# Weight sums of a seven-product multiplication made by adding DMA transfers: one decoder layer on one core

## The chip, the cores and the metric

The kernel runs on one core of a Trainium2 chip. A core has five engines with a queue of instructions each: TensorE (PE, matrix products into PSUM), VectorE (DVE), ScalarE (ACT), GpSimd (POOL) and SyncE (SP), and 16 DMA engines that they share. SP and POOL start the DMA transfers in this kernel. The metric is the device time of one execution in microseconds (us); lower is better.

## What is computed

One decoder layer on 512 tokens of 2048 features, in float32. A normed input is projected to 6664 features; three groups work on these (a convolution, a "forgetting" attention of 8 heads, a memory attention of 4 heads); their gated outputs, 2048 features together, go through the output projection, a residual and a norm.

```python
h = rmsnorm(x, norm_g[l])
proj = h @ w_in[l]
(cv_a, cv_b, cv_gate, fq, fk, fv, f_logit, fox_gate, mq, mem_gate) = jnp.split(proj, SPLITS, axis=-1)
...
y_fox = fox_attention(fq.reshape(shp), fk.reshape(shp), fv.reshape(shp), logf)   # causal, 8 heads of 128
y_fox = y_fox * jax.nn.silu(fox_gate)
...
y = jnp.concatenate([y_conv, y_fox, y_mem], axis=-1)
x = x + y @ w_out[l]
return rmsnorm(x, final_g)
```

## The kernel before

PE multiplies reduced float32 (`F32R`), which keeps too few bits, so each operand is split into a high and a low part: `split` casts on ACT (line 93, `whi`) and takes the remainder on DVE (line 94, `wlo`). A product of two operands is then three matmuls (high x high, high x low, low x high). `operand` does this for a weight tile `raw` of [128, 8, 128] floats (512 KB), with three buffers for each of `whi` and `wlo` and six for `raw`.

The stages follow one another: the start (memory keys and values, norm, transposes of `h`), the convolution and the memory attention, then the eight heads of the forgetting attention, then the output projection.

**The pair stage.** A head needs four blocks of 128 features, worked on as two pairs: query and key, then gate and value. The first pair (`plain_pair`) is multiplied as it is. The other 15 (`pair`, lines 711 to 759) use Winograd's form of Strassen's scheme: the 2x2 block product of weights (two feature blocks `fa`, `fb` by two halves of the 2048 rows) and `h` (two halves of the features by two halves of the tokens) is done in seven half-size products instead of eight. Each of the seven (`product`) is 24 matmuls of 256 columns on sums of blocks. The sums of `h`'s quarters, `s1` to `s4`, are made once (`first_sums`, `last_sum`). The sums of weights are made for every pair: four plain loads on SP's queue (line 719) fetch the blocks `b11`, `b12`, `b22`, `b21`, and `less` (line 703) takes four differences on DVE. The three PSUM tiles `x1`, `zo`, `x2` gather the results: a product adds onto what lies in its tile, and between products DVE adds to a tile (`plus`, line 700) or ACT copies it away (`kept`, line 707).

A pair is a generator of three steps. The main loop runs a pair's first step, then the previous pair's last product and attention work, then the pair's second step, so that attention overlaps the next pair's products. A scheduler that the framework runs at build time orders each engine's queue by its own estimates; what it did is shown with the change. Attention's masks (line 796) run on POOL, which also starts the DMA that writes a head's finished output `yd` (line 833).

**The output steps.** The output projection works by eight steps, `STEPS`: four "y" steps (plain products of the convolution's and the memory's parts) and four "s" steps (`heads`, the heads' parts in the same seven-product form, with sums of `y`'s quarters made by `head_ys`). An "s" step loads four tiles of `w_out` (`next_piece`) and takes the same four differences on DVE by line 703. Its matmuls are line 981; results are added onto `res` by `add` (line 907).

Of the kernel before, what the change touches and what calls it, by code (L numbers as in the profile page):

```python
# [17 lines left out]
P = 128  # L18
S = 512
# [28 lines left out]
def hybrid_layer_kernel(  # L48
# [41 lines left out]
    def split(hi, lo, src, scale=None):  # L90
        """hi + lo == src (times scale): twelve significant bits each."""
        if scale is None:
            ins = nc.scalar.copy(hi, src)  # L93
            nc.vector.tensor_tensor(lo, src, hi.bitcast(F32), ALU.subtract)  # L94
        else:
            ins = nc.scalar.activation(hi, src, AF.Identity, scale=scale)
            nc.vector.scalar_tensor_tensor(
                lo, src, scale, hi.bitcast(F32), ALU.mult, ALU.subtract
            )
        return ins.ins  # L100
# [6 lines left out]

    bg = deque()
# [8 lines left out]
    def operand(src, out=None):  # L117
        """src [P, n, c], whole -> its two parts."""
        if out is None:
            out = tuple(  # L120
                wp.tile(list(src.shape), F32R, tag=t, name=nm(t), bufs=3) for t in ("whi", "wlo")
            )
        split(*out, src)
        return out

    def weights(src, n, c, raw=None, hold=None):
        """src [n * P, c] -> k -> (hi, lo) of its k-th P rows."""
        half = n // 2
# [23 lines left out]
    # x normed, [feature, token], two features' tiles in each  # L152
# [12 lines left out]
    # ---- start: memory values and keys (rows transposed as they come, their  # L165
    # norm applied to the results), x normed and transposed ----
# [130 lines left out]
    def project(f0, per=0):  # L297
        """[P features from f0, tokens] in PSUM."""
        w = weights(w_in[:, f0 : f0 + P], KT, P)
        o = pj()  # L300
        for k in range(KT):
            mm3(o, w(k), (h_hi[k], h_lo[k]), k == 0, k == KT - 1)
        background(per)
        return o

    def silu_of(pool, o, tag, bufs):
        """silu of a PSUM tile."""
        sg = pool.tile([P, S], F32, tag=tag, name=nm(tag), bufs=bufs)
# [5 lines left out]
    NC = CW // P  # L314
    PAD = TAPS - 1
    with tc.tile_pool(name="conv", bufs=1, reuse_waits="tile") as cp:
# [151 lines left out]
        with tc.tile_pool(name="matt", bufs=1, reuse_waits="tile") as ma:  # L468
            # the channel norm's sums and the gates run between the heads
# [68 lines left out]
        # sums of h's quarters (token halves by feature halves); the last takes  # L538
        # the place of the quarter that no product needs
# [22 lines left out]
        def first_sums(g):  # L562
            t1, t2, t3 = tmp("t1"), tmp("t2"), tmp("t3")
            whole(t1, quarter(g, 0, 1))
            whole(t2, quarter(g, 1, 1))
            nc.vector.tensor_tensor(t2, t1, t2, ALU.add)
            split(*sums[0][g], t2)
            whole(t3, quarter(g, 0, 0))
            nc.vector.tensor_tensor(t1, t3, t1, ALU.subtract)
            split(*sums[2][g], t1)  # L570
            nc.vector.tensor_tensor(t2, t2, t3, ALU.subtract)
            split(*sums[1][g], t2)

        def last_sum(g, t1, t2):
            whole(t1, quarter(g, 1, 0))
            whole(t2, sums[1][g])
            nc.vector.tensor_tensor(t1, t1, t2, ALU.subtract)
            split(*quarter(g, 0, 1), t1)
# [18 lines left out]
    # ---- the output projection's operands; what they need of the room of h and  # L597
    # its sums falls free with the last pair's products. The convolution's and
    # the memory's parts of y are multiplied as they are; the heads' parts by the
    # same form as the pairs, with sums of their quarters (token halves by halves  # L600
    # of the heads) ----
# [14 lines left out]
    def w_pieces():  # L616
        for kind, n in STEPS:
            c0 = n * S
            if kind == "s":
                for k0, c in ((4, c0), (4, c0 + M), (8, c0 + M), (8, c0)):  # L620
                    yield w_rows(k0, HK, c, M), HK, M
            else:
                for k0 in (0, 2, 12, 14):
                    yield w_rows(k0, 2, c0, S), 2, S
# [33 lines left out]
    def head_ys(j, fa, fb):  # L658
        """Heads j and 4 + j, whole: their quarters' parts and those of the
        sums, which take the room of fa and fb."""  # L660
# [15 lines left out]
        nc.vector.tensor_tensor(a22, a21, a22, ALU.add)  # L676
        split(*q["s1"], a22)
        nc.vector.tensor_tensor(a22, a22, a11, ALU.subtract)
# [3 lines left out]
        nc.vector.tensor_tensor(a12, a12, a22, ALU.subtract)  # L682
# [4 lines left out]
    with tc.tile_pool(name="fox", bufs=1, reuse_waits="tile") as fx:  # L687
# [14 lines left out]
        def less(o, p, q):  # L702
            nc.vector.tensor_tensor(o, p, q, ALU.subtract)  # L703

# [5 lines left out]
        def pair(fa, fb):  # L710
            """Features fa.. and fb.., P each, by Winograd's form of Strassen's
            seven products: the first in PSUM, by token halves, the second in
            SBUF. In three steps, for another pair's to come between."""
            HK = KT // 2

            def load(f0, half):
                r = raw_tile(HK, P)
                rows = slice(half * HK * P, (half + 1) * HK * P)
                nc.sync.dma_start(
                    out=r, in_=w_in[rows, f0 : f0 + P].rearrange("(k p) f -> p k f", p=P)  # L720
                )
                return r

            # Sums are taken in PSUM: a product adds onto what its bank holds,
            # which copies and an addition have read or changed before. Only a
            # bank's first product starts afresh.
# [10 lines left out]
            b11, b12, b22, b21 = load(fa, 0), load(fb, 0), load(fb, 1), load(fa, 1)  # L737
            x1, zo, x2 = (pj((P, M)) for _ in range(3))
            product(x1, b11, a11, start=True)
            yield  # L740
            p1 = kept(x1, "p1")
            less(b11, b12, b11)
            product(zo, b11, s1, start=True)
            p5 = kept(zo, "p5")
            less(b11, b22, b11)
            product(x2, b11, s2, start=True)
            plus(x2, x2, p1)
            u2 = kept(x2, "u2")
            product(x1, b21, a12)
            product(zo, b22, s4)  # L750
            less(b12, b22, b12)
            product(x2, b12, s3)
            col = fx.tile([P, S], F32, tag="col", name=nm("col"), bufs=2)
            plus(col[:, M:], x2, p5)
            plus(col[:, :M], zo, u2)
            less(b21, b21, b11)
            yield
            product(x2, b21, a22)
# [130 lines left out]
    head_ys(3, heads[6], last_y)  # L889
    with tc.tile_pool(name="outp", bufs=1, reuse_waits="tile") as op:  # L890
# [4 lines left out]
        # by token halves and column blocks  # L895
# [12 lines left out]

        ALL = slice(0, S)
# [9 lines left out]
        def sides(n):  # L919
            """y's other parts; the last time, a token tile at a time and to the end."""  # L920
# [20 lines left out]
            for t in range(NT):  # L941
# [3 lines left out]
                # the very last one by halves, for less to follow its products  # L945
# [40 lines left out]
        def heads(n):  # L986
            b11, b12, b22, b21 = (next_piece() for _ in range(4))
            x1, zo, x2 = (pj((P, 2, M)) for _ in range(3))
            r11, r12, r21, r22 = (
                res[h][n][:, :, c * M : (c + 1) * M] for h in range(2) for c in range(2)  # L990
            )
            product(x1, b11, "a11", start=True)
            yield
            p1 = y_room(n % 2).rearrange("p (t f) -> p t f", f=M)
            nc.scalar.copy(p1, x1)
            less(b11, b12, b11)
            product(zo, b11, "s1", start=True)
            add(r22, zo)
            less(b11, b22, b11)
            product(x2, b11, "s2", start=True)  # L1000
            add(x2, p1)
            add(r12, x2)
            product(zo, b22, "s4")
            add(r12, zo)
            less(b12, b22, b12)
            product(x1, b21, "a12")
            add(r11, x1)
            product(x2, b12, "s3")
            add(r22, x2)
            less(b21, b21, b11)  # L1010
            yield
            product(x2, b21, "a22")
            add(r21, x2)
# [66 lines left out]
```

## Time and profile before

| what | value |
|---|---|
| median of 3 runs | 870.68 us (870.58 to 870.77) |
| the profiled execution: span, first to last instruction | 868.8 us |
| PE busy | 855.3 us (98%) |
| DVE busy | 704.8 us (81%) |
| ACT busy | 436.2 us (50%) |
| POOL busy | 45.1 us (5%) |
| hardware DMA queue | 102.52 MB, 39.3% of 16 engines |
| software DMA queue (POOL's) | 4.11 MB, 1.3% of 16 engines |
| granted TensorE clock | 0.996 |

The profiled execution's own device time isn't listed apart from the runs; beside its span of 868.8 us stands their median. In the rows of the profile, "L703 DVE TENSOR_TENSOR raw<-raw,raw" is an instruction of line 703 on DVE that reads two `raw` tiles and writes one; "x76 | 92.7, 1220 | 0.5" is 76 of them, 92.7 us busy, 1220 ns each, 0.5 us of idle time of the engine before them. Rows of waits read "who waits <- for what: us in total, times, longest". A DMA's "took" is the issue on its engine; "to landing" is from issue to the arrival of the data. A row of windows gives start and end, the length, then each engine's busy time, the granted clock, the mean busy share of the DMA engines and GB/s.

### The profile page before, as it was taken

To read this page: it belongs to the slowest core of one execution; us is meant where nothing else is said; L and a number is where in the kernel's file an instruction comes from. 1 tells how busy PE (TensorE), PEld (TensorE's weight loads), DVE (VectorE), ACT (ScalarE), POOL (GpSimd) and SP (SyncE) were. 2 spreads that over 40 slices of the span, in tenths; PEclk is the share of its full clock that TensorE was granted. 3 is DMA by queue.
4 is the path that set the end of the run, shared out by engine and by line. 5 is a ranking of instruction groups with operands and counts; after the bars stand their busy time and mean duration, and the time that the engine had idled before them with its cause. 6 is when DMAs were issued, how large, how long until landed. Compare 5 with 4: busy or idle time off the path is not lost.

```text
span 868.8 us, 14045 instructions
## 1 busy us (share of the span) xinstructions
PE 855.3 (98%) x5562; PEld 775.1 (89%) x5562; DVE 704.8 (81%) x1051; ACT 436.2 (50%) x679; POOL 45.1 (5%) x76
## 2 busy tenths in 40 slices
PE   8999999999999999999999999999999999999996
PEld 6897887888888888999999999999999888998995
DVE  4686799999977998998787878878797886876964
ACT  4874322224346544566565555656464852443523
POOL 1011000000000002010101010101010000000001
PEclk9999999999999999999999999999999999999999
DMA  9972233333332333233434243333334627351415
GB/s 323 356 197 76 70 82 105 97 97 89 94 85 85 109 90 117 79 106 109 121 93 127 74 120 101 107 103 91 107 84 146 239 73 267 97 195 49 146 49 194
DMA packets 143265, 107.52 MB, mean 124 GB/s; under 512 B 3892, under 2 KB 126816, under 8 KB 142560
## 3 DMA queue, kind: packets, MB, share of 16 engines
q1 hardware_dynamic: 141696, 102.52, 39.3%
q0 software_dynamic: 1504, 4.11, 1.3%
q8 instruction: 43, 0.70, 0.3%
q14 instruction: 22, 0.18, 0.1%
HBM read 98.46 MB, written 8.14 MB: 123 GB/s over the span
## 4 chain that ended last, share of the span: by engine, by line
PE 95%; issue 1%; ACT 1%; DVE 1%; DMA 1%; SPq 0%; POOL 0%; POOLq 0%; ACTq 0%
PE pj L732 33%; PE pj L104 13%; PE pj L105 13%; PE pj L106 13%; PE pj L981 8%; PE at L104 3%; PE at L105 3%; PE at L106 3%; PE at L820 1%; DMA raw<-in_w_mem_kv_dram 1%; PE pj L409 0%; PE pj L408 0%; PE pj L262 0%; PE at L262 0%; PE at L782 0%
## 5 line engine op out<-in xcount | busy, mean ns | idle before, releaser
L93 ACT CAST whi<-raw 128x1024 fp32r<-128x1024 f32 x205 | 215.1, 1051 | 324.2 <-PE pj L105 110.9
L94 DVE TENSOR_TENSOR wlo<-raw,whi 128x1024 fp32r<-128x1024 f32 x205 | 250.1, 1221 | 87.5 <-ACT whi L93 86.6
L105 PE MATMUL pj<-hl,whi 128*128 128x512 f32 x352 | 139.6, 397 | 0.0
L106 PE MATMUL pj<-hh,wlo 128*128 128x512 f32 x352 | 139.1, 396 | 0.0
L104 PE MATMUL pj<-hh,whi 128*128 128x512 f32 x352 | 138.9, 396 | 0.0
L732 PE MATMUL pj<-hh,wlo 128*128 128x256 f32 x480 | 135.0, 281 | 0.0
L732 PE MATMUL pj<-hl,whi 128*128 128x256 f32 x480 | 134.9, 281 | 0.0
L732 PE MATMUL pj<-hh,whi 128*128 128x256 f32 x480 | 134.8, 281 | 0.0
L703 DVE TENSOR_TENSOR raw<-raw,raw 128x1024 f32<-128x1024 f32 x76 | 92.7, 1220 | 0.5
L732 PEld LDWEIGHTS pj<-hl,whi 128*128 128x128 f32 x480 | 90.4, 188 | 0.1
L732 PEld LDWEIGHTS pj<-hh,whi 128*128 128x128 f32 x480 | 90.5, 188 | 0.0
L732 PEld LDWEIGHTS pj<-hh,wlo 128*128 128x128 f32 x480 | 90.4, 188 | 0.0
L329 DVE SCALAR_TENSOR_TENSOR acc<-up,cwt,acc 128x512 f32<-128x512 f32 x120 | 85.2, 741 | 0.4
L981 PE MATMUL pj<-whi,rh 128*128 128x256 f32 x448 | 80.0, 280 | 0.7 <-DVE sst L1035 0.4
L104 PEld LDWEIGHTS pj<-hh,whi 128*128 128x128 f32 x352 | 66.1, 188 | 15.9 <-PE pj L262 0.2
L106 PEld LDWEIGHTS pj<-hh,wlo 128*128 128x128 f32 x352 | 66.1, 188 | 15.7
L105 PEld LDWEIGHTS pj<-hl,whi 128*128 128x128 f32 x352 | 66.1, 188 | 15.5
L981 PEld LDWEIGHTS pj<-whi,rh 128*128 128x128 f32 x448 | 68.8, 188 | 1.3 <-DVE res L907 1.1
L981 PE MATMUL pj<-wlo,rh 128*128 128x256 f32 x224 | 62.3, 279 | 0.0
L981 PEld LDWEIGHTS pj<-wlo,rh 128*128 128x128 f32 x224 | 42.1, 188 | 0.2
L796 POOL TENSOR_SCALAR_AFFINE_SELECT b<-b 128x128 f32<-128x128 f32 x32 | 21.3, 676 | 265.6 <-ACT b L795 234.0
L732 PE MATMUL pj<-s0h,whi 128*128 128x256 f32 x120 | 34.9, 291 | 0.0
(302 smaller groups left out, 1720.5 us busy)
## 6 DMA issues: line engine op xcount, KB each, us to landing
raw<-in_w_in_dram SPq DMA_DIRECT2D x104, 512.0 KB, 3.6
raw<-in_w_out_dram SPq DMA_DIRECT2D x32, 512.0 KB, 4.5
raw<-in_w_mem_kv_dram SPq DMA_DIRECT2D x12, 512.0 KB, 7.3
xr<-in_x_dram SPq DMA_DIRECT2D x4, 1024.0 KB, 7.8
res<-in_x_dram SPq DMA_DIRECT2D x8, 512.0 KB, 6.8
out_dram<-res SPq DMA_DIRECT2D x16, 256.0 KB, 2.8
rs<-yd SPq DMA_DIRECT2D x15, 256.0 KB, 4.6
mr<-in_mem_dram SPq DMA_DIRECT2D x8, 256.0 KB, 7.2
```

The costliest lines, as they stand in the source:

```text
L93: ins = nc.scalar.copy(hi, src)
L94: nc.vector.tensor_tensor(lo, src, hi.bitcast(F32), ALU.subtract)
L104: nc.tensor.matmul(o, ah, bh, start=start, stop=False)
L105: nc.tensor.matmul(o, ah, bl, start=False, stop=False)
L106: nc.tensor.matmul(o, al, bh, start=False, stop=stop)
L329: return lambda: nc.vector.scalar_tensor_tensor(a, up[:, j : j + S], cwt[:, c, j : j + 1], a, ALU.mult, ALU.add)
L703: nc.vector.tensor_tensor(o, p, q, ALU.subtract)
L732: nc.tensor.matmul(o, p[:, k, :], q, start=start and k == 0 and i == 0, stop=k == HK - 1 and i == 2, skip_group_check=True,)
L796: nc.gpsimd.affine_select(out=b[:, sl], in_=b[:, sl], pattern=[[-1, P]], compare_op=ALU.is_ge, fill=MASKED, base=0, channel_multiplier=1,)
L820: nc.tensor.transpose(tp[:, (i - j) * P : (i - j + 1) * P], pr[i][:, j * P : (j + 1) * P], ident)
L981: nc.tensor.matmul(o[:, m, :], p, q[:, k, :], start=start and k + m + i == 0, stop=k == HK - 1 and i == 2, skip_group_check=True,)
```

## The change

The sums of weights are no longer made on DVE. A tile is loaded plainly, and then further blocks are fetched by DMA transfers that add onto it in SBUF (`accum_op=ALU.add`, on POOL's queue). Since only adding is used, all weight sums have plus signs: one tile, `chain`, is in turn the first block, plus a second, plus a third, plus a fourth; another, `r22`, gets one addition. The signs of the sums of `h` and `y` and of some PSUM steps change to match (`negated_less`, `take`). Blocks that were loaded once and used in several sums are fetched anew for each sum: beside 60 plain loads of the pairs (line 726 after) come 60 adding ones (line 730 after), beside 16 of the output steps 16 more (line 1003 after). The products are reordered: from a11, s1, s2, a12, s4, s3, a22 to s1, a11, s4, s2, a12, s3, a22, so that between two uses of the chain's tile lie products that use other tiles. `less` is gone. The number of PE's instructions is the same.

```diff
+    def negated_less(o, p, q):
+        nc.vector.scalar_tensor_tensor(o, p, -1.0, q, ALU.mult, ALU.subtract)
...
-            nc.vector.tensor_tensor(t2, t1, t2, ALU.add)
+            nc.vector.tensor_tensor(t2, t2, t1, ALU.subtract)
...
-                for k0, c in ((4, c0), (4, c0 + M), (8, c0 + M), (8, c0)):
+                for k0, c in ((4, c0), (4, c0), (8, c0 + M), (8, c0)):
...
         def pair(fa, fb):
+            def rows(f0, half):
+                r = slice(half * HK * P, (half + 1) * HK * P)
+                return w_in[r, f0 : f0 + P].rearrange("(k p) f -> p k f", p=P)
...
+            def plus_weights(r, f0, half):
+                nc.gpsimd.dma_start(out=r, in_=rows(f0, half), accum_op=ALU.add)
...
-            b11, b12, b22, b21 = load(fa, 0), load(fb, 0), load(fb, 1), load(fa, 1)
+            chain, r11 = load(fa, 0), load(fa, 0)
+            plus_weights(chain, fb, 0)
+            r22, r21 = load(fb, 1), load(fa, 1)
             x1, zo, x2 = (pj((P, M)) for _ in range(3))
-            product(x1, b11, a11, start=True)
+            product(zo, chain, s1, start=True)
             yield
+            plus_weights(chain, fb, 1)
+            p5 = kept(zo, "p5")
+            product(x1, r11, a11, start=True)
             p1 = kept(x1, "p1")
-            less(b11, b12, b11)
-            product(zo, b11, s1, start=True)
-            p5 = kept(zo, "p5")
-            less(b11, b22, b11)
-            product(x2, b11, s2, start=True)
+            product(zo, r22, s4)
+            plus_weights(r22, fb, 0)
+            product(x2, chain, s2, start=True)
+            plus_weights(chain, fa, 1)
             plus(x2, x2, p1)
             u2 = kept(x2, "u2")
-            product(x1, b21, a12)
-            product(zo, b22, s4)
-            less(b12, b22, b12)
-            product(x2, b12, s3)
             col = fx.tile([P, S], F32, tag="col", name=nm("col"), bufs=2)
-            plus(col[:, M:], x2, p5)
-            plus(col[:, :M], zo, u2)
-            less(b21, b21, b11)
+            negated_less(col[:, :M], zo, u2)
+            product(x1, r21, a12)
+            product(x2, r22, s3)
+            negated_less(col[:, M:], x2, p5)
             yield
-            product(x2, b21, a22)
+            product(x2, chain, a22)
             yield (x1, x2), col
...
         def heads(n):
-            b11, b12, b22, b21 = (next_piece() for _ in range(4))
+            chain, r1, r2, r3 = (next_piece() for _ in range(4))
+            c0 = n * S
+
+            def plus_weights(r, k0, c):
+                nc.gpsimd.dma_start(out=r, in_=w_rows(k0, HK, c, M), accum_op=ALU.add)
...
+            plus_weights(chain, 4, c0 + M)
+            product(zo, chain, "s1", start=True)
+            take(r22, zo)
             yield
+            plus_weights(chain, 8, c0 + M)
+            product(x1, r1, "a11", start=True)
...
+            product(zo, r2, "s4")
+            take(r12, zo)
+            plus_weights(r2, 4, c0 + M)
+            product(x2, chain, "s2", start=True)
+            plus_weights(chain, 8, c0)
             add(x2, p1)
-            add(r12, x2)
...
+            take(r12, x2)
+            product(x1, r3, "a12")
             add(r11, x1)
-            product(x2, b12, "s3")
-            add(r22, x2)
-            less(b21, b21, b11)
+            product(x2, r2, "s3")
+            take(r22, x2)
             yield
-            product(x2, b21, "a22")
+            product(x2, chain, "a22")
             add(r21, x2)
```

First place: POOL's queue in the pair stage, about one head (two pairs) of it. Before, it holds a head's four masks and the write of the head's output:

```order
L796 AFFINE_SELECT b_4190<-b_4190 128x128
L796 AFFINE_SELECT b_4206<-b_4206 128x128
L796 AFFINE_SELECT b_4222<-b_4222 128x128
L796 AFFINE_SELECT b_4238<-b_4238 128x128
L833 DMA yd_68<-fgate_3906 128x512
```

After, the same queue; `raw_4408` is the chain of a pair of queries and keys and `raw_4413` its `r22`, `raw_4111` and `raw_4116` are those of the pair before, `raw_4680` and `raw_4977` the chains of the next two:

```order
L730 DMA raw_4408<-in_w_in_dram 128x8x128
L730 DMA raw_4111<-in_w_in_dram 128x8x128
L730 DMA raw_4116<-in_w_in_dram 128x8x128
L730 DMA raw_4111<-in_w_in_dram 128x8x128
L730 DMA raw_4680<-in_w_in_dram 128x8x128
L730 DMA raw_4408<-in_w_in_dram 128x8x128
L730 DMA raw_4413<-in_w_in_dram 128x8x128
L805 AFFINE_SELECT b_4760<-b_4760 128x128
L730 DMA raw_4408<-in_w_in_dram 128x8x128
L805 AFFINE_SELECT b_4776<-b_4776 128x128
L805 AFFINE_SELECT b_4792<-b_4792 128x128
L805 AFFINE_SELECT b_4808<-b_4808 128x128
```

A chain's first sum now stands ahead of the second and third sums of the pair before, and the masks stand between sums.

Second place: DVE's queue in the pair stage. Before, with `raw_4408`, `raw_4410`, `raw_4412` and `raw_4414` the blocks b11, b12, b22 and b21 of one pair, and `fgate`, `ptl` and `vl` attention's tiles:

```order
L703 TENSOR_TENSOR raw_4408<-raw_4410,raw_4408 128x1024
L94 TENSOR_TENSOR wlo_4448<-raw_4117,whi_4447 128x1024
L703 TENSOR_TENSOR raw_4410<-raw_4412,raw_4410 128x1024
L700 TENSOR_TENSOR col_4404<-pj_4121,p_577_4285 128x256
L94 TENSOR_TENSOR wlo_4530<-raw_4408,whi_4529 128x1024
L703 TENSOR_TENSOR raw_4408<-raw_4412,raw_4408 128x1024
L94 TENSOR_TENSOR ptl_2843<-at_4490,pth_2839 128x512
L94 TENSOR_TENSOR ptl_2844<-at_4497,pth_2840 128x384
L94 TENSOR_TENSOR wlo_4561<-raw_4408,whi_4560 128x1024
```

After, for the same pair (`raw_4408` the chain, `raw_4410` r11, `raw_4413` r22, `raw_4415` r21):

```order
L94 TENSOR_TENSOR wlo_4531<-raw_4410,whi_4530 128x1024
L94 TENSOR_TENSOR wlo_4561<-raw_4413,whi_4560 128x1024
L94 TENSOR_TENSOR wlo_4590<-raw_4408,whi_4589 128x1024
L787 TENSOR_TENSOR fgate_4476<-pj_4122,fgate_4476 128x256
L94 TENSOR_TENSOR vl_4487<-at_4481,vh_4486 128x512
L94 TENSOR_TENSOR ptl_2843<-at_4491,pth_2839 128x512
L94 TENSOR_TENSOR ptl_2844<-at_4498,pth_2840 128x384
L94 TENSOR_TENSOR wlo_4624<-raw_4415,whi_4623 128x1024
L94 TENSOR_TENSOR ptl_2845<-at_4504,pth_2841 128x256
L94 TENSOR_TENSOR ptl_2846<-at_4509,pth_2842 128x128
L94 TENSOR_TENSOR wlo_4652<-raw_4413,whi_4651 128x1024
```

The sums between the remainders are gone; the remainders now follow the new order of products (a11, s4, s2, a12, s3), and one DVE row of attention and then the addition onto `x2` (line 704 after) come behind the last row shown, the remainder for s3.

More of the change, by code (lines that the diff above doesn't have):

```diff
@@ L570, in first_sums @@
             split(*sums[2][g], t1)
-            nc.vector.tensor_tensor(t2, t2, t3, ALU.subtract)
+            negated_less(t2, t2, t3)
             split(*sums[1][g], t2)
@@ L576, in last_sum @@
             whole(t2, sums[1][g])
-            nc.vector.tensor_tensor(t1, t1, t2, ALU.subtract)
+            negated_less(t1, t2, t1)
             split(*quarter(g, 0, 1), t1)
@@ L675, in head_ys @@
         split(*(t[:, 1, :] for t in base), fb)
-        nc.vector.tensor_tensor(a22, a21, a22, ALU.add)
+        nc.vector.tensor_tensor(a22, a22, a21, ALU.subtract)
         split(*q["s1"], a22)
-        nc.vector.tensor_tensor(a22, a22, a11, ALU.subtract)
+        negated_less(a22, a22, a11)
         split(*q["s2"], a22)
@@ L681, in head_ys @@
         split(*q["s3"], a21)
-        nc.vector.tensor_tensor(a12, a12, a22, ALU.subtract)
+        negated_less(a12, a22, a12)
         split(*q["s4"], a12)
@@ L700, in plus @@
             nc.vector.tensor_tensor(o, p, q, ALU.add)
-        def less(o, p, q):
-            nc.vector.tensor_tensor(o, p, q, ALU.subtract)
         def kept(src, tag):
@@ L714, in pair @@
             HK = KT // 2
+            def rows(f0, half):
+                r = slice(half * HK * P, (half + 1) * HK * P)
+                return w_in[r, f0 : f0 + P].rearrange("(k p) f -> p k f", p=P)
             def load(f0, half):
                 r = raw_tile(HK, P)
[L718 to L721, printed above, removed]
-                return r
+                nc.sync.dma_start(out=r, in_=rows(f0, half))
+                return r
+            def plus_weights(r, f0, half):
+                nc.gpsimd.dma_start(out=r, in_=rows(f0, half), accum_op=ALU.add)
             def product(o, w, a, start=False):
@@ L907, in add, with take @@
             nc.vector.tensor_tensor(o, o, p, ALU.add)
+        def take(o, p):
+            nc.vector.tensor_tensor(o, o, p, ALU.subtract)
         ALL = slice(0, S)
@@ L991, in heads @@
             )
-            product(x1, b11, "a11", start=True)
+            plus_weights(chain, 4, c0 + M)
+            product(zo, chain, "s1", start=True)
+            take(r22, zo)
             yield
+            plus_weights(chain, 8, c0 + M)
+            product(x1, r1, "a11", start=True)
             p1 = y_room(n % 2).rearrange("p (t f) -> p t f", f=M)
             nc.scalar.copy(p1, x1)
[L996 to L1000, printed above, removed]
-            add(x2, p1)
-            add(r12, x2)
[L1003 to L1006, printed above, removed]
+            product(zo, r2, "s4")
[3 more added lines that the diff above has]
+            plus_weights(chain, 8, c0)
+            add(x2, p1)
+            take(r12, x2)
+            product(x1, r3, "a12")
             add(r11, x1)
-            product(x2, b12, "s3")
-            add(r22, x2)
-            less(b21, b21, b11)
+            product(x2, r2, "s3")
+            take(r22, x2)
             yield
-            product(x2, b21, "a22")
+            product(x2, chain, "a22")
             add(r21, x2)
```

## The prediction

> **What bounds the kernel now.** I read the page's shares and slices first, then the chain, then what the tensor engine waits for, then two windows in the stages that the change touches.
>
> ```profile
> span 868.8 us, 14045 instructions
> PE 855.3 (98%) x5562; PEld 775.1 (89%) x5562; DVE 704.8 (81%) x1051; ACT 436.2 (50%) x679; POOL 45.1 (5%) x76
> PE 95%; issue 1%; ACT 1%; DVE 1%; DMA 1%; SPq 0%; POOL 0%; POOLq 0%; ACTq 0%
> PE pj L104 <- ACT mh L96: 2.4, 1, 2.4
> PE at L177 <- POOL ident masks.py:199: 1.4, 1, 1.4
> PE pj L104 <- ACT whi L93: 0.6, 1, 0.6
> PE pj L981 <- DVE sst L1035: 0.4, 1, 0.4
> PE pj L981 <- DVE res L907: 0.3, 1, 0.3
> PE at L234 <- DMA mr<-in_mem_dram: 0.2, 1, 0.2
> PE pj L732 <- DVE wlo L94: 0.2, 1, 0.2
> ```
>
> TensorE (PE) is busy for 98% of the span and makes up 95% of the chain that ended last. The last seven rows are all of its waits: 5.5 us. The two longest, 3.8 us together, and the 0.2 us for `mr` belong to the start, which the change leaves alone. What is left is 1.5 us, and no row names a weight sum (line 703): its output never arrives last.
>
> A head in the pair stage (two pairs) takes 45.15 us; the third row is an output step:
>
> ```profile
> core 0: us, PE busy (x) PEld busy (x) DVE busy (x) ACT busy (x) POOL busy (x), PEclk, DMA share, GB/s
> 448.97:494.12 45.15, 45.15 (x377) 44.89 (x376) 37.55 (x55) 26.75 (x45) 3.25 (x5) 1.00 0.38 105
> 494.12:539.28 45.16, 45.16 (x377) 44.90 (x376) 37.54 (x55) 26.77 (x45) 3.25 (x5) 1.00 0.39 106
> 735.00:770.00 35.00, 34.72 (x292) 34.30 (x291) 30.21 (x34) 16.08 (x22) 0.00 (x0) 1.00 0.28 91
> ```
>
> PE is filled in the pairs to the last hundredth, VectorE (DVE) to 83%, and the 16 DMA engines to 0.385. From the chain in the same place:
>
> ```profile
> 473.62 13.84 PE pj L732 x117
> ```
>
> One 256-column matmul takes 13.84/117 = 118.3 ns there, a product of 24 takes 2.84 us, and seven take 19.9 of a pair's 22.6 us; the other 2.7 us are attention. PE's instructions are the same number after the change, so the pair stage is no shorter unless this 118.3 ns falls, and longer only if an operand comes late.
>
> **The change, part by part.** These rows carry the prices:
>
> ```profile
> L703 DVE TENSOR_TENSOR raw<-raw,raw 128x1024 f32<-128x1024 f32 x76 | 92.7, 1220 | 0.5
> L94 DVE TENSOR_TENSOR wlo<-raw,whi 128x1024 fp32r<-128x1024 f32 x205 | 250.1, 1221 | 87.5 <-ACT whi L93 86.6
> L93 ACT CAST whi<-raw 128x1024 fp32r<-128x1024 f32 x205 | 215.1, 1051 | 324.2 <-PE pj L105 110.9
> L700 DVE TENSOR_TENSOR pj<-pj,p 128x256 f32<-128x256 f32 x2 | 0.9, 428 | 1.4 <-PE pj L732 1.4
> L707 ACT COPY u<-pj 128x256 f32<-128x256 f32 x2 | 0.7, 364 | 0.9 <-DVE pj L700 0.9
> q1 hardware_dynamic: 8386, 4.42, 35.6%
> L719 SPq DMA_DIRECT2D raw<-in_w_in_dram x60: 367/368/744, 306.6 to 651.7; - x60
> DMA to landing us min/median/max: 3.4/3.7/5.8
> L833 POOL DMA_DIRECT2D yd<-fgate x7: 560/560/560, 390.1 to 655.5; - x7
> DMA to landing us min/median/max: 2.5/3.3/4.9
> L400 POOL DMA_DIRECT2D wf<-in_w_in_dram x1: 1230/1230/1230, 74.1 to 74.1; - x1
> DMA to landing us min/median/max: 5.2/5.2/5.2
> ```
>
> *Removed.* All 76 sums of line 703 leave DVE: 76 x 1.22 = 92.7 us, of which 8 x 1.22 = 9.8 us lie in one head; DVE there falls from 37.55 to about 27.8 of 45.15 us. None of it lies on the path, so it brings 0. At most it brings the waits of changed code, 1.5 us, if a DVE with more room would close them all.
>
> *Added.* 76 DMA transfers on GpSimd's (POOL's) queue, each of 512 KB in 512-byte pieces, which read the weights from memory and add them onto the tile that lies in SBUF: four per pair, four per output step of the seven-product form. Plain loads stay four per pair. Three prices are to be found, and the trace holds no transfer that adds.
>
> (a) POOL's time per issue. `yd` (128 pieces) took 560 ns and `wf` (2048 pieces of 32 bytes) 1230 ns. Between them by pieces, 1024 cost 560 + 896 x 670/1920 = 0.87 us; ends 0.56 and 1.23. Eight per head are 7 us beside 3.25 us of masks: POOL stays under a quarter full. Cost 0.
>
> (b) The engines' time. The hardware queue's row is of the head's window 448.97 to 494.12: 35.6% of 45.15 is 16.1 us for 4.42 MB, so 3.64 us per MB and 1.91 us for a 512 KB load (0.524 MB). Below, an adding transfer costs no less than the load it contains: 1.91 us. Above, it handles three streams of that size (memory read, SBUF read, SBUF write) one after the other: 3 x 1.91 = 5.7 us. The head has 45.15 - 0.385 x 45.15 = 27.8 us free, so eight transfers fit up to 3.47 us each, 1.82 times a load. I take 2.9 us (1.5 times): the load's row is nearest, with the same bytes and pieces, and the second read overlaps in part. That makes 17.4 + 23.2 = 40.6 of 45.15 us: hidden, but not by much. Cost 0; at the ends 0, and 17.4 + 45.8 - 45.15 = 18 us per head, which is +135 us over 7.5 heads. The Trainium skill, "Collectives: The Full Stack", section "The bandwidth ceiling", says that a transfer that adds needs two source reads on one ring and so runs at half the rate of a copy (62.28 against 32.35 GB/s in its measurement). By that rule the eight transfers would not fit; no run so far shows it.
>
> (c) The time from issue to landing, which counts where an adding transfer waits for the splitting of the tile and the next product waits for the transfer. A load lands after 3.7 us; with one more passage of 1.9 us and POOL's longer issue I take 6.2 us; ends 3.7 (a load's) and 8.9 (3.7 + 5.2, the two slowest medians in a row). The rooms, with product p's splitting possible only after product p - 3 (three buffers), and 2.84 us each: the sum onto r22 is issued when s4 is split, about 2.6 us after the start of the preceding pair's a22, and s3 starts at 16.9 us. Before s3 come its own cast and remainder (1.05 + 1.22), and the room of an addition and a copy (0.43 + 0.36) with signals: it must land by 13.5. Room 10.9 us. The chain's third sum (for a22) has 13.6 us, its second 13.0 us, its first is a pair ahead. All exceed 8.9. Cost 0.
>
> *Queue order.* On POOL the mask of the next head's first block now stands behind two sums that wait for splits, and three more masks behind a third. Masks are 0.68 us each and are needed only in the next pair's attention, so a wait of some microseconds costs 0; if cover fails there, attention's 2.7 us per pair of PE work comes late. On SP the loads are as many; the chain's tile is held longer, and a load waits for another slot, but the first sum of a pair is issued a whole pair (22.6 us) before its product.
>
> *Product order.* s1 first, and only a12 (2.84 us) between s2 and s3 instead of a12 and s4. In that gap come the addition onto `x2` and the copy `u`: 0.43 + 0.36 = 0.8 us and two signals. With DVE at 60% it fits. Cost 0; if DVE is in the middle of a remainder, 1.2 us more, still under 2.84.
>
> *Signs.* Two subtractions per pair become scalar_tensor_tensor on DVE. A 416 ns addition may become 450; beside other work. In the output steps `take` for `add` is the same instruction. Cost 0.
>
> *Output steps.* Before, 0.28 of DMA in the window of one step. Four transfers add 4 x 1.9 to 2.9 us per step to about 25 us: under 0.7. Cost 0; the two waits (0.4 and 0.3) may go.
>
> Sum: 0, between -1.5 and whatever (b) or (c) take if they overflow. The profiled execution has a span of 868.8 us; the shown runs have a median of 870.68, so 1.9 us lie around the span. 868.8 + 1.9 - 0.2 for a part of the closing waits = **870.5 us**. Runs of before lie within 0.1 us of their median; I call 0.2% (1.74 us) the least difference to be told from none.
>
> **The rivals.**
>
> *DMA becomes the bound (slower).* If an adding transfer holds its engines for twice a load, as one that reads twice would, the head needs 17.4 + 8 x 3.82 = 48.0 us: +2.8 us x 7.5 heads = +21, **891 us**. It decides from 3.47 us per transfer (1.82 times); at 2.15 times it is 908. For it: two reads per byte, and pieces of 512 bytes that already cost a load 1.91 us; the margin at twice is negative by 6% only. Against it: reading and writing may overlap. This is the case that the page cited at (b) would make. Chance 0.33.
>
> *The r22 sum lands late (slower).* The chain is then split of s4, issue on POOL, landing, split for s3, and PE stands before s3 in every pair. Each us over 10.9 costs 15 us; at 12 us to landing +17, **888 us**. For it: descriptors made on POOL one after another, two sums that can be issued back to back and then share the engines. Against: the room is 1.75 times my estimate. The Trainium skill, "SBUF — State Buffer", section "SBUF: two separate sides", warns that POOL cannot write descriptors while DVE runs an operation with both ports; the seven `yd` issues took 560 ns each, beside a DVE that is busy 83%, which shows none of it. Chance 0.12.
>
> *Faster.* The matmul's 118.3 ns may owe something to DVE's traffic in SBUF. The output step shows:
>
> ```profile
> 736.31 14.01 PE pj L981 x120
> ```
>
> That is 116.8 ns, though DVE is busy for 86% there. So a busier DVE goes with a shorter matmul, against the idea; were it true, 15 x 168 x 1.5 ns = 3.8 us would go: **866.9 us**. Closing all 1.5 us of waits alone would stay under the bound of telling. Chance 0.07.
>
> *Small losses (slower).* `x2` is ready late before s3 in some pairs, or masks are: 0.2 us x 15 = 3 us, **873.5 us**. For: the gap is halved. Against: DVE has 22% more of its time free. Chance 0.07.
>
> **How the numbers follow.** Hidden, no change that can be told: 0.41, the likeliest single case. DMA bound 0.33, late sum 0.12, small losses 0.07: slower 0.52. Faster 0.07. Predicted time 870.5. The range starts at 868.8, where the removable waits are nearly all gone, which leaves out about 0.06; it ends at 908 (adding transfers at 2.15 times a load, or a late sum at 13.4 us), which leaves out about 0.13. The likeliest case alone spans 869 to 872.4.
>
> **What would show it.** Right: DVE near 612 us, no line of sums, a new row of 60 issues on POOL with about 6 us to landing, DMA share 0.8 to 0.9 in a head's window of 45.15 us, PE's waits still under 0.6 us each. For the DMA bound: slices of DMA at 9 all through the pairs, heads longer than 45.2 us, loads (not only sums) landing far later than 3.7 us, PE waiting for `wlo` of any product. For the late sum: waits of PE only before s3, DMA share below 0.8. What would make the prediction wrong is above all (b): a price per transfer that I have no row for.

## The result: 7.4% slower, and the profile after

The changed kernel takes 935.96 us (median of 4 runs, 932.06 to 939.68) against 870.72 us before: ratio 1.0745, 95% interval 1.0715 to 1.0775. The forecast was 870.5 us, in a range that ended at 908.

First the page's shares, the chain and all of PE's waits, as they were shown of before:

```profile
span 934.5 us, 14154 instructions
PE 876.3 (94%) x5562; PEld 793.3 (85%) x5562; DVE 627.3 (67%) x975; ACT 429.0 (46%) x677; POOL 155.0 (17%) x152
PE 58%; DMA 24%; ACT 7%; issue 5%; DVE 4%; POOL 1%; ACTq 0%; POOLq 0%; SPq 0%; DVEq 0%
PE at L829 <- DVE vl L94: 30.2, 7, 4.9
PE at L104 <- ACT fq L93: 10.1, 6, 3.3
PE pj L740 <- ACT u L708: 5.8, 1, 5.8
PE pj L104 <- ACT mh L96: 2.2, 1, 2.2
PE at L181 <- POOL ident masks.py:199: 1.4, 1, 1.4
PE pj L105 <- DVE wlo L94: 0.2, 1, 0.2
```

PE's share of the chain fell from 95% to 58%, and DMA has 24%. Yet no wait of PE names a weight sum. PE waits for attention's operands: seven times, in seven heads, 30.2 us together for `vl`, and six times for `fq`. The 5.8 us for `u` are one wait, before s3 of the last pair.

Where the time lies is read from the first and last start of the matmuls of the pairs (lines 732 and 740) and of the output steps (981 and 993); the two numbers behind the durations are these starts. Before:

```profile
L732 PE MATMUL pj<-hh,whi x480: 277/280/365, 348.7 to 695.1; 128*128 128x256 f32 x160
L981 PE MATMUL pj<-whi,rh x448: 276/280/390, 736.1 to 844.7; 128*128 128x256 f32 x150
```

After:

```profile
L740 PE MATMUL pj<-s0h,whi x120: 277/280/285, 349.2 to 724.4; 128*128 128x256 f32 x120
L740 PE MATMUL pj<-hh,whi x480: 277/281/416, 352.0 to 761.3; 128*128 128x256 f32 x160
L993 PE MATMUL pj<-whi,rh x448: 277/280/283, 802.7 to 910.0; 128*128 128x256 f32 x150
```

The pairs take 412.1 us (349.2 to 761.3) instead of 346.4. That is 65.7 us, the whole loss. The output steps take 107.3 instead of 108.6: their 16 adding transfers cost nothing in this kernel. A head, two pairs, shows what else grew:

```profile
core 0: us, PE busy (x) PEld busy (x) DVE busy (x) ACT busy (x) POOL busy (x), PEclk, DMA share, GB/s
449.07:501.00 51.93, 47.22 (x377) 46.41 (x376) 29.48 (x47) 26.26 (x44) 14.20 (x13) 0.97 1.01 173
501.00:555.60 54.60, 47.73 (x376) 46.93 (x375) 29.48 (x47) 26.24 (x44) 15.87 (x14) 0.94 0.96 164
```

DVE fell from 37.55 to 29.5 us; the forecast was 27.8. A head takes 52 to 55 us instead of 45.2; 4.7 to 6.9 us of it PE stands idle, and another 2.1 to 2.6 us it is busy for longer at a lower granted clock. The DMA share of 0.96 to 1.01 looks as if the DMA engines were full. The rows of the adding transfers:

```profile
q0 software_dynamic: 72352, 43.96, 35.4%
raw<-in_w_in_dram POOLq DMA_DIRECT2D x60, 512.0 KB, 7.9
L730 POOL DMA_DIRECT2D raw<-in_w_in_dram x60: 1540/1549/2262, 311.5 to 730.7; - x60
DMA to landing us min/median/max: 6.5/7.9/13.5
```

35.4% of 934.5 us, less the 11.3 us that this queue took before (1.3% of 868.8), are 319 us over 76 transfers: 4.2 us each, 2.2 times a load. By that price eight transfers and the rest of a head need 17.4 + 33.6 = 51 us, just about what a head takes. The plain loads of the pairs, too, land after a median of 5.6 us instead of 3.7, which the forecast had named as a sign of this. This is one reading, theory A: the DMA engines are the bound.

The chain in one head tells another (start, length, what):

```profile
473.95 0.40 ACT fgate L786
474.34 0.02 issue
474.37 0.43 DVE fgate L787
474.80 0.58 POOL raw L730
475.39 0.29 issue
475.68 11.44 DMA raw<-in_w_in_dram
487.11 0.02 issue
...
487.21 0.10 ACT whi L93
487.31 0.15 issue
...
488.16 0.38 ACT fgate L786
488.54 0.47 ACT vh L93
```

At 474.80 POOL issues the first sum of the *next* pair (`raw_4680` of the order shown above), whose plain load had landed at 474.00; that load itself had waited for a slot of `raw` until 469.57. (The chain names `fgate` for this release, because that operation ended at 474.80; for the next pair's first sum, issued at 501.08, it names the load, which landed 0.63 us before.) Only behind it, at 475.68, goes the second sum of *this* pair, although the splitting of s1, which it must follow, was done by 471.9 (cast at 469.23, remainder at 470.71). It lands 11.4 us later. ACT's queue at the same time (start, busy, what, and in brackets the idle time before):

```profile
477.22 1.05 ACT L93 CAST whi<-raw 128x1024 fp32r<-128x1024 f32 x1 [1.50 <-PE pj L740]
478.18 0.36 ACT L708 COPY p<-pj 128x256 f32<-128x256 f32 x1
487.21 1.04 ACT L93 CAST whi<-raw 128x1024 fp32r<-128x1024 f32 x1 [8.68 <-DMA raw<-in_w_in_dram]
488.16 0.38 ACT L786 ACTIVATE fgate<-pj 128x256 f32<-128x256 f32 x1
488.44 0.58 ACT L93 CAST vh<-at 128x512 fp32r<-128x512 f32 x1
```

ACT stands for 8.68 us at the cast for s2, and behind it are attention's gate and values (`fgate`, `vh`), whose own inputs were there. PE, which has s4 and then attention ahead of s2, runs dry at 486.2. Theory B: the engines have room, but the order on POOL issues the second sum late, and ACT's order makes attention late with it.

### The profile page after: what moved, and what is told of

Its sections match the earlier page's. It is cut to its first block, busy times and chain, and to the rows that moved or that the text cites. A ratio compares the mean times of both kernels' runs of the same rounds, so it can differ in the third digit from the quotient of the medians.

```text
span 934.5 us, 14154 instructions
## 1 busy us (share of the span) xinstructions
PE 876.3 (94%) x5562; PEld 793.3 (85%) x5562; DVE 627.3 (67%) x975; ACT 429.0 (46%) x677; POOL 155.0 (17%) x152
## 3 DMA queue, kind: packets, MB, share of 16 engines
q0 software_dynamic: 72352, 43.96, 35.4%
## 4 chain that ended last, share of the span: by engine, by line
PE 58%; DMA 24%; ACT 7%; issue 5%; DVE 4%; POOL 1%; ACTq 0%; POOLq 0%; SPq 0%; DVEq 0%
DMA raw<-in_w_in_dram 24%; PE pj L105 12%; PE pj L106 12%; PE pj L104 12%; PE pj L993 8%; PE pj L740 3%; ACT whi L93 3%; DVE wlo L94 2%; PE at L104 2%; PE at L106 2%; PE at L105 2%; POOL raw L730 1%; ACT b L804 1%; ACT pth L93 1%; DVE b L812 1%
## 5 line engine op out<-in xcount | busy, mean ns | idle before, releaser
L740 PE MATMUL pj<-hh,wlo 128*128 128x256 f32 x480 | 140.0, 292 | 0.0
L740 PE MATMUL pj<-hh,whi 128*128 128x256 f32 x480 | 138.3, 288 | 0.0
L740 PE MATMUL pj<-hl,whi 128*128 128x256 f32 x480 | 137.0, 285 | 0.0
L730 POOL DMA_DIRECT2D raw<-in_w_in_dram x60 | 93.4, 1700 | 209.7 <-DVE wlo L94 72.2
L740 PEld LDWEIGHTS pj<-hh,wlo 128*128 128x128 f32 x480 | 93.7, 195 | 0.3
L740 PEld LDWEIGHTS pj<-hl,whi 128*128 128x128 f32 x480 | 92.9, 194 | 0.4
L740 PEld LDWEIGHTS pj<-hh,whi 128*128 128x128 f32 x480 | 92.9, 193 | 0.4
L104 PEld LDWEIGHTS pj<-hh,whi 128*128 128x128 f32 x352 | 66.1, 188 | 15.8 <-PE pj L266 0.2
L105 PEld LDWEIGHTS pj<-hl,whi 128*128 128x128 f32 x352 | 66.1, 188 | 15.6
L106 PEld LDWEIGHTS pj<-hh,wlo 128*128 128x128 f32 x352 | 66.2, 188 | 15.6
L1003 POOL DMA_DIRECT2D raw<-in_w_out_dram x16 | 20.5, 1282 | 140.7 <-DMA raw<-in_w_out_dram 76.7
L829 PE MATMUL at<-ident,b 128*128 128x128 f32 x80 | 15.1, 308 | 30.2 <-DVE vl L94 30.2
```

The costliest lines, as they stand in the source:

```text
L104: nc.tensor.matmul(o, ah, bh, start=start, stop=False)
L105: nc.tensor.matmul(o, ah, bl, start=False, stop=False)
L106: nc.tensor.matmul(o, al, bh, start=False, stop=stop)
L730: nc.gpsimd.dma_start(out=r, in_=rows(f0, half), accum_op=ALU.add)
L740: nc.tensor.matmul(o, p[:, k, :], q, start=start and k == 0 and i == 0, stop=k == HK - 1 and i == 2, skip_group_check=True,)
L829: nc.tensor.transpose(tp[:, (i - j) * P : (i - j + 1) * P], pr[i][:, j * P : (j + 1) * P], ident)
```

## The experiments

**1. Prices.**

> This kernel leaves out the layer and only moves weights into eight tiles of 512 KB, phase by phase: eight plain loads from SP, eight plain ones from POOL, eight adding ones from POOL, one of each alone, eight plain and eight adding in pieces of 2 KB, four adding beside four plain, and eight adding beside a busy DVE. Theory A (the DMA engines are full): adding transfers land about 4.2 us apart when nothing else runs, the price that the share of the software queue gives in the changed kernel (319 us over 76). Theory B (an order of queues makes them late): they land 2 to 3 us apart, so that eight of them and the rest of a head (17.4 us) would fit into 45 us, and the 4.2 us hold waiting in them. Both: one alone lands after about 6 us, a plain load after 3.5.

The eight adding transfers land, as seen from a tiny DVE operation on each tile (start, busy, and in brackets the wait for the landing), first and last of eight:

```profile
42.85 0.16 DVE L94 TENSOR_TENSOR sums<-sums,raw 128x1 f32<-128x1 f32 x1 [6.59 <-DMA raw<-in_w_in_dram]
...
63.98 0.16 DVE L94 TENSOR_TENSOR sums<-sums,raw 128x1 f32<-128x1 f32 x1 [2.75 <-DMA raw<-in_w_in_dram]
```

(63.98 - 42.85)/7 = 3.02 us each. The plain loads on the same queue came 1.81 us apart (22.98 to 33.82 in six steps), with the same pieces; an adding one costs 1.67 times a load. The prices add up when both kinds run at once: of four loads and four adding transfers together, the last landed 17.8 us after the first, and three loads and four adding ones come to 17.5. One alone landed after 6.3 us, a plain one on POOL after 4.5 and on SP after 3.9. In the windows of eight adding transfers, alone and beside a busy DVE:

```profile
36.00:64.00 28.00, 1.40 (x13) 12.54 (x8) 1.00 1.21 150
147.00:175.00 28.00, 15.15 (x29) 12.52 (x8) 1.00 1.21 150
```

The columns are DVE, POOL, clock, DMA share, GB/s. DVE's work (15.15 us) changes nothing. And the share is 1.21 with nothing but these transfers: for adding transfers this column is not a share that ends at 1, and the 4.2 us worked out from it are too many. With 3.02 us, eight and the rest are 17.4 + 24.2 = 41.6 of 45.15 us: they fit. The measured spacing is at the upper end of theory B's 2 to 3 us.

**2. Overwriting instead of adding.**

```diff
-                nc.gpsimd.dma_start(out=r, in_=rows(f0, half), accum_op=ALU.add)
+                nc.gpsimd.dma_start(out=r, in_=rows(f0, half))
```

(and the same in the output steps).

> The 76 transfers of POOL's queue overwrite instead of adding, so the weight sums are left out; same bytes, pieces, order, splits and waits. Theory A: 17.4 + 8 x 1.9 = 32.7 us of DMA in a head, so no loss is left: 870 to 873 us. Theory B: the second sums still wait behind the next pair's first, but land some 4 to 5.5 us after issue instead of 8 to 11: most of the loss goes, 870 to 885 us. If the loss comes from POOL's 1.5 us per issue or from the order alone: over 915 us.

869.07 us, ratio 0.998 (0.9971 to 0.9990), a little under both ranges. The 60 transfers land after 4.3 us instead of 7.9:

```profile
raw<-in_w_in_dram POOLq DMA_DIRECT2D x60, 512.0 KB, 4.3
```

PE waits for nothing in the pairs. So the new order costs nothing by itself: it takes the adding transfer's slowness too. It doesn't part A from B. Nor does it clear POOL's time per issue, for an overwriting transfer keeps POOL for 0.88 us and an adding one for 1.55; run 4, with 1.55, does that.

**3. Adding transfers for which nobody waits.** In the pairs s1 takes `r11`, and s2, s3 and a22 take `r21`.

> The pairs' 60 adding transfers run as before, but no product uses their tiles: s1 takes r11, s2, s3 and a22 take r21, so four of the seven weight sums are left out. The DMA engines have the same work. Theory A: a head needs at least 17.4 + 8 x 4.2 = 51 us of DMA, and loads come late: 915 us or more. Theory B: nothing late is waited for: 870 to 880 us.

969.98 us, ratio 1.1136 (1.1119 to 1.1153): slower than the change itself, which reads like A. But the run doesn't test what it was meant to. With no splits between them a chain's three sums wait for each other's landing, and they do so at the head of POOL's queue:

```profile
  DMA raw<-in_w_in_dram: 317.9, 43
```

This row is of POOL's idle time ahead of line 730: 317.9 us in 43 waits for a landing, of which 164.5 us in 30 waits are for an adding transfer and the rest for plain loads. Which of the things queued behind, masks or later sums, then held up PE was not followed further.

**4. The second sum ahead of the next pair's first.** Two rows of POOL's queue change places; the order of everything else is the same.

```diff
...
-            plus_weights(chain, fb, 0)
+            with tc.issue_after(seconds[-1].ins) if seconds else ExitStack():
+                plus_weights(chain, fb, 0)
...
-            plus_weights(chain, fb, 1)
+            seconds.append(plus_weights(chain, fb, 1))
```

> On POOL's queue a pair's first adding transfer is issued behind the second one of the pair before, instead of ahead of it; the rest of the order is unchanged. Theory A: the same transfers in another order, 930 to 940 us. Theory B: the second sum is issued about 4 us earlier and not back to back with another, the seven waits of about 4.7 us before attention's transposes shrink to under 1 us: 895 to 910 us.

875.41 us, ratio 1.0066 (1.0040 to 1.0091). The swap gives back 60 of 65 us, more than B had put on it, whose range began at 895. A head of this run:

```profile
450.20:495.40 45.20, 45.20 (x377) 44.93 (x376) 29.98 (x48) 26.66 (x44) 14.26 (x13) 1.00 1.14 199
L732 POOL DMA_DIRECT2D raw<-in_w_in_dram x60: 1540/1548/2269, 312.5 to 672.3; - x60
DMA to landing us min/median/max: 6.7/8.7/12.9
456.68 3.14 POOL L732 DMA_DIRECT2D raw<-in_w_in_dram  x2 [8.79 <-DVE col L110]
PE pj L742 <- ACT u L708: 3.5, 1, 3.5
```

(line 732 is the adding transfer in this kernel, 742 the pairs' matmul.) 45.20 us with PE busy throughout, the same 60 transfers, a median landing of 8.7 us, no shorter than in the changed kernel. The plain loads of the pairs land after a median of 7.3 us, later than the 5.6 of the changed kernel, and PE waits for none: late loads were no sign of a DMA bound. Theory A falls. In the head of the same pairs the second sum was issued at 456.68, the first of the two in that row, 0.1 us before s3's matmuls began (456.79), against 4.0 us after (475.68 and 471.70) in the changed kernel, and it landed after 6.7 us, since the slower place, second of two, is now the next first sum's, which has time. So the swap brings it 4.1 us by issue and 4.7 by landing. Only one wait above 0.5 us is left in the pairs, 3.5 us at the last pair.

**5. The output steps alone.** The pairs, signs of `h`'s sums and DVE sums of before; the output steps of the change.

> The kernel before, with the 16 adding transfers, the new order of products and the new signs in the output steps alone; the pairs as before. Theory B: in the output steps the sums land in time, and the first to the last output matmul took 1.0 us less after the change than before (123.4 against 124.4 us): 869 to 871 us. If adding transfers cost something wherever they are: at least 16/76 of the 65 us, 884 us.

875.1 us, ratio 1.0053 (1.0042 to 1.0065): a miss. The rows of PE's waits and the chain:

```profile
PE pj L987 <- ACT whi L93: 3.2, 1, 3.2
PE pj L987 <- DVE wlo L94: 2.4, 2, 1.7
738.48 10.32 DMA raw<-in_w_out_dram
748.89 1.05 ACT whi L93
```

A second sum is late again, once, but not by the order on POOL: the first step's second sum was issued at 738.48, 0.3 us after the remainder of s1, which it must follow, had ended. That was 2.3 us after the first output matmul (736.16), and it took 10.3 us to land. In the changed kernel the same transfer was issued 0.5 us ahead of that matmul (802.18 against 802.66) and landed after 6.0. Here s1 itself was split late: its own sum, issued at 724.16, took 9.8 us and landed 2.2 us ahead of the first output matmul, in the changed kernel 5.7 us. So the output steps are free only where their sums happen to be issued early.

**6. The new order with sums on DVE.**

```diff
-            chain, r11 = load(fa, 0), load(fa, 0)
-            plus_weights(chain, fb, 0)
-            r22, r21 = load(fb, 1), load(fa, 1)
+            r11, r12, r22, r21 = load(fa, 0), load(fb, 0), load(fb, 1), load(fa, 1)
+            chain = raw_tile(HK, P)
+            plus(chain, r11, r12)
...
-            plus_weights(chain, fb, 1)
+            plus(chain, chain, r22)
...
```

(and likewise for the other two sums).

> The changed kernel with the pairs' four weight sums made on DVE again, from a fifth tile per pair; new order of products, new signs and the output steps stay. Theory B: order and signs cost nothing: 869 to 872 us. If the new order is to blame (a shorter way from s2 to s3, a fifth tile short of slots): over 880 us.

871.53 us, ratio 1.0007 (0.9998 to 1.0015). Product order, signs, and the halved gap from s2 to s3 cost nothing to speak of: the forecast had those at 0.

**7. Run 4 with the last pair's late sum on DVE.** From an extra load in the last pair alone.

```diff
...
+            r12 = load(fb, 0) if last else r22
...
-            plus_weights(r22, fb, 0)
+            plus(r12, r12, r22) if last else plus_weights(r22, fb, 0)
...
-            plus_weights(chain, fa, 1)
+            plus(chain, chain, r21) if last else plus_weights(chain, fa, 1)
...
```

> As the run with the second sum ahead of the next first, and in the last pair alone two of the four sums (the one for s3, from an extra load, and the one for a22) are made on DVE. That run had one wait left in the pairs, 3.8 us before the last pair's s3. Theory B: it goes, 869 to 872 us, level with the overwriting kernel. If its 4.5 us over the kernel before lie in the adding itself: 874 to 876 us.

870.02 us beside 871.0 before, ratio 0.9992 (0.9983 to 1.0000). The last wait is gone: PE waits for nothing after the start. This is the best full version found, and it is level with the kernel before, or 0.1% faster, with 58 of 60 adding transfers still in the pairs.

**8. ACT's cast behind attention.** The cast for s2 is issued behind the casts of the attention before it.

```diff
...
-            product(x2, chain, s2, start=True)
+            with tc.issue_after(ahead_on_act[0]) if ahead_on_act[0] else ExitStack():
+                product(x2, chain, s2, start=True)
...
```

> The changed kernel with ACT's cast for s2 issued behind the casts of the attention before it; the sums are as late as they were for one pair in two (the order on POOL is moved for the other as well). Theory B with ACT's queue as multiplier: the seven waits of about 4.7 us before attention's transposes fall under 1.5 us each, and some of the lateness shows as waits before s2 instead: 885 to 910 us. If ACT's order is unimportant: the same waits in full before s2, 925 us or more.

900.67 us, ratio 1.0339 (1.0323 to 1.0355).

```profile
PE pj L742 <- DVE col L110: 17.4, 7, 3.7
```

The seven waits for `vl` are gone; in their place PE waits seven times, 2.5 us on average, before a22 and not before s2 as forecast. The row names DVE's `col`, but a late sum stands behind it. In the wait that ended at 498.40, ACT had stood 6.66 us at the cast for a22 until the chain's third sum, issued at 484.84, landed at 495.19; the remainder and then `col` followed on DVE. That third sum had to follow the splitting of s2, and s2's own sum, issued at 468.66, had taken 13.4 us. This run gives back 35 of the 65 us, and not all of that is ACT's order, since the scheduler swapped two rows on POOL for every other pair with it, as in run 4: the six waits for `fq`, 10.1 us, went with the swapped pairs. In the pairs that kept their order on POOL, 30.2 us of waits became 17.4. So ACT's order matters, and how much of the 35 us is its share stays open.

**9. Two sums of four on DVE.** The chain's second and third sums from tiles that are loaded anyway.

```diff
-            plus_weights(chain, fb, 1)
+            plus(chain, chain, r22)
...
-            plus_weights(chain, fa, 1)
+            plus(chain, chain, r21)
```

> The changed kernel with the chain's second and third sums made on DVE, from the tiles r22 and r21 that are loaded anyway; the chain's first sum and the sum onto r22 stay adding transfers, and the first one of the next pair still stands ahead of the r22 sum on POOL. Theory B: no adding transfer is left whose room is shorter than its queue and landing, but r22's, with 10.9 us; at some 7 us to landing and 1 to 3 us behind the other it is in time: 869 to 873 us. If it is late in every pair as the second sum was: over 885 us.

871.61 us beside 870.63, ratio 1.0010 (1.0001 to 1.0019). The sum onto `r22`, on which the forecast's rival had put the lateness, is in time in all pairs but the last (one wait of 1.4 us), with the next first sum still ahead of it. What was late were the chain's own sums. This run takes two of them off at once; that the second is the one follows from run 4, which moved it alone, and from ACT's wait for it in the changed kernel.

## Why the prediction was wrong, point by point

- *What bounds the kernel.* Right: nothing was to be gained from DVE. With the 76 sums off DVE and none late (run 2) the kernel is 0.2% faster, 1.8 us, about the 1.5 us of waits that the forecast named as the most. DVE's busy time falls less than the forecast had it, from 704.8 to 628.4 us in that run and 627.3 in the changed kernel, not to 612; why was not followed.
- *(a) POOL's issue.* Taken 0.87 us, ends 0.56 and 1.23; measured 1.54, and 2.26 for the second of two in a row. Outside the ends, and POOL was 27 to 29% full in a head, not under a quarter; still no bound by itself, as run 4 shows.
- *(b) The engines' time.* Taken 2.9 us, measured 3.02 by run 1. The forecast's step held, in part by luck: the load was priced at 1.91 us where run 1 has 1.81, and the factor was 1.5 where it has 1.67. The rival that DMA becomes the bound, with the highest chance among those that lose, did not happen: eight fit, as run 4's heads of 45.2 us show. The Trainium skill's rule cited there ("Collectives: The Full Stack", section "The bandwidth ceiling"), half the rate, would have made 3.6 us of a 1.81 us load. The measurement, 3.02 us, is 1.67 times a load: the rule, which the page gives for rings between cores, is too dear by a fifth here.
- *(c) The failing step.* The room of the chain's second sum was given as 13.0 us. With s2 at 3 x 2.84 + 2.7 = 11.2 us after a22's start, less its cast, its remainder and signals, the limit is 8.7 us after a22's start, so the room supposes an issue 4.3 us ahead of a22, soon after s1's splitting. The order printed with the change shows the next pair's first sum ahead of it. I looked at the first sum's own deadline, a whole pair away, and did not ask what it makes the transfers behind it wait for: its plain load, and for that a `raw` slot that only s3's splitting frees. By the trace the issue came 1.6 us ahead of a22 (475.68 against 477.28). The second part of the step, 6.2 us to landing with 8.9 as the upper end, came out as 6.5 to 13.5, and 11.4 in this place: two adding transfers back to back share the engines, as the eight of run 1 did, where each that follows lands 3 us later. Issue and landing together: 9.8 us after a22's start, where 8.7 was the limit.
- *Queue order, costed at 0.* On these numbers s2 alone would have been some 1 us late. What made the wait of 4.4 us of it is ACT's queue: attention's casts stand behind the cast for s2. The forecast asked what stands behind a wait on POOL and SP, not on ACT, where the splitting of the summed tile itself waits. Its limit should have been the time at which the cast reaches the head of ACT's queue, here 478.54, not the start of s2.
- *The rival of a late sum* (chance 0.12, 888 us) was the right kind. It named the wrong sum, onto r22, and left out ACT.
- *A loss without a term.* After a wait PE is slower for a while. The stretch behind the wait that ended at 490.60, 4.4 us long, and a longer one in which PE has work:

```profile
490.60:494.40 3.80, 3.80 (x17) 3.49 (x18) 2.67 (x5) 3.68 (x7) 2.83 (x4) 0.60 0.60 65
494.40:506.00 11.60, 11.60 (x98) 11.60 (x98) 6.63 (x9) 4.21 (x6) 3.73 (x3) 0.98 0.86 189
```

  The granted clock is 0.60 for 3.8 us and 0.98 behind that. PE is busy 876.3 us instead of 855.3 for the same instructions: 21 of the 66 us. The Trainium skill, "TensorE: Matmul & The Clock Gate", section "What's actually happening", says that the array falls to half its clock after an idle window of about 3.4 us and needs about as long to come back; the 4.4 us wait and the 3.8 us agree with it. In run 8 the clock fell behind a wait of 3.7 us (first row) and stayed behind one of 2.7 us (second row):

```profile
447.51:451.30 3.79, 3.79 (x18) 3.79 (x19) 2.72 (x3) 1.72 (x3) 2.25 (x2) 0.50 0.83 182
498.40:502.20 3.80, 3.80 (x32) 3.80 (x33) 2.98 (x5) 2.41 (x5) 2.26 (x2) 1.00 0.96 209
```

## What to carry to other kernels

When a transfer is put on an in-order queue, its room is to be counted from when the transfers ahead of it in the printed order can go, and those wait for their own loads and slots; a swap of two rows was worth 60 us here. Ask also on every engine that waits for the transfer what stands behind that wait: the deadline is when the waiting instruction reaches the head of its queue, not when its result is needed. And taking work off an engine that nobody waits for brings next to nothing: 76 sums off DVE, 76 us of its busy time, were worth at most 1.8 us.

## What the runs showed of the hardware

An adding transfer of 512 KB costs 3.02 us of the DMA engines against 1.81 for a plain one in 512-byte pieces, and 2.58 against 1.44 in pieces of 2 KB (run 1). Its issue alone keeps POOL for 1.54 us with 1024 pieces of 512 bytes (an overwriting one for 0.88 in run 2) and for 1.28 with 512 pieces of 1 KB. The busy share of the DMA engines goes above 1 with adding transfers (1.21 with them alone), so it can't be read as how full the engines are: at 1.01 in the changed kernel they seemed to be the bound, and at 1.14 in run 4 they were not.
